# ACT copies the gate's products out of PSUM, and the sums of squares at the changes of layer go to TensorE

## The chip, the cores and the metric

The kernel runs on one core of a Trainium2 chip, in one launch. The metric is device time in microseconds (us), the median of three runs. The core has five engines that work beside each other, each through its own instructions in a fixed order: TensorE (PE in the profile; PEld is its weight load), VectorE (DVE), ScalarE (ACT), GpSimd (POOL), and SyncE (SP), which issues the DMAs. TensorE writes into PSUM, and DVE and ACT read it there.

## The reference

Two blocks follow one another on a sequence of 512 positions with 1024 channels. The first has two layers of feed-forward, mixer, feed-forward. The second has an even layer (rwkv, on 256 context positions and the 512 main ones) and an odd layer (retention). Cut to what the change touches:

```python
def rmsnorm(x, g):
    xf = x.astype(jnp.float32)
    y = xf * lax.rsqrt(jnp.mean(xf * xf, axis=-1, keepdims=True) + EPS)
    return (y * g.astype(jnp.float32)).astype(x.dtype)
...
# second_block, per layer; first_block ends each sublayer likewise
hl = rmsnorm(xl, norm_pre[layer]) * (1.0 + scale_l[:, None, :]) + shift_l[:, None, :]
hc = rmsnorm(xc, norm_pre[layer]) * (1.0 + scale_c) + shift_c
oc, ol = even_mixer(hc, hl, ...)      # odd_mixer in the odd layer
xl = xl + gate_l[:, None, :] * rmsnorm(ol, norm_post[layer])
if need_ctx:
    xc = xc + gate_c * rmsnorm(oc, norm_post[layer])
...
# even_mixer: u = h @ w_in gives r, k0, v, gate_r, four, gate_f
yr = o.astype(gate_r.dtype) * jax.nn.silu(gate_r)
yf = fourier_mix(four) * jax.nn.silu(gate_f)
return jnp.concatenate([yr, yf], axis=-1) @ w_out
```

## The kernel before

Channels lie on partitions: x is 8 tiles of 128x512, the context 8 tiles of 128x256 (`xc`). Every product runs in split precision: ACT copies a weight's high part (`whi`, L169), DVE subtracts to get the low part (`wlo`, L253), and three products are added up in PSUM (hi by hi, lo by hi, hi by lo; L174 records them all).

The **even layer** takes the most stages here. Its normed input is `ehh`/`ehl`, 768 columns wide (256 context, then 512 main). A projection of 128 channels (`project_in`, L999) fills one PSUM tile for the context columns (`ipc`, 128x256) and one for the main ones (`ipm`, 128x512). There is one buffer of each, so the next projection's first product into `ipc` waits until the last reader of this one has read. For each of six pairs of heads there are four projections: v, r and k0 (`shifted`, L1022, which lets ACT copy `ipc` and `ipm` into an SBUF tile `u` of 128x768, with one buffer, and mixes neighbours from there) and the gate (`project_gate`, L1347). The gate's silu is `sg = (tanh(g/2) + 1) * g`: ACT takes two tanh out of PSUM, and two DVE instructions add one and multiply by `ipc` and `ipm`, again out of PSUM. `sg` lies in one of the SBUF buffers that r, k and v share (tag `rkv`). Two more calls serve the Fourier channels, eight in all.

The recurrence itself runs in 12 slots, two directions for each pair. A slot's chain goes over all engines: a triangular inverse on DVE (`un`, `tmp`, L1508 to L1522: 28 short additions, each on the one before), a trip by DMA into `blocks`, transposes on DVE (`tn`, L1538), products `p`, `pb`, `ch` and so on. The projections (dense work) are laid between the chain's small products to fill TensorE. The order is set by a scheduler that plays the program on a timeline model when it is built, and then stands fixed on every engine.

At a **change of layer** the output y of a half (256 columns) is normed, scaled and added to x: `residual` (L389) does y's scaling on DVE (L188), the addition on POOL (L402), a square on ACT (`sq`) and, where a layer of the next block follows, the sum of squares on DVE (`sumsq`, L355: one addition of 128x256 into `xacc`, `xcacc` or `xkeep` for every tile but the first). The next layer's `norm_in` (L903) then calls `rstd_bc` (L331): products of the sum with ones into `st_ps`, ACT's square root, DVE's reciprocal, and products with the identity that spread the result over the partitions (`bc`). At the changes of sublayer within the first block `residual` already does it otherwise: each `sq` goes through products with ones into two PSUM columns (`xs`), with no addition on DVE. Such changes happen at about 420 us and later in the first block; the change from first to second block is near 2000 us, the one from the even to the odd layer near 2970 us.

Of the kernel before, what the change touches and what calls it, by code (L numbers as in the profile page):

```python
# [8 lines left out]
F32 = mybir.dt.float32  # L9
F32R = mybir.dt.float32r  # L10
AF = mybir.ActivationFunctionType
ALU = mybir.AluOpType
PSUM = bass.MemoryType.PSUM

D = 1024
KD = 8
# [132 lines left out]
class K:  # L149
# [236 lines left out]
        self.act(y[o][:, cols], ps[:, cols], AF.Copy)  # L386
        self.sumsq(yacc, ps[:, cols], o == 0, cols)

    def residual(self, x, y, yacc, c0, n, G, xacc=None, last=False):  # L389

        cols = slice(c0, c0 + n)
        bc = self.rstd_bc(yacc, c0, n, 1.0 / D, self.eps6)
        gates = list(zip(self.PEG, self.stats))
        sums = [self.paux("xs", *self.NST) for _ in range(2)] if xacc is None and not last else []
        done = None
        for k in range(KD + 1):
            if k < KD:
                with self.tc.issue_after(done.ins) if done and not self.POOLX else nullcontext():
                    self.stt(y[k][:, cols], y[k][:, cols], G[:, k : k + 1], bc[:, cols])
            if k:  # L400
                new = x[k - 1][:, cols]
                done = (self.nc.vector if last and k % 2 == 0 and (c0 or k > 4) else self.nc.gpsimd).tensor_tensor(out=new, in0=new, in1=y[k - 1][:, cols], op=ALU.add)  # L402
                if xacc is not None:
                    self.sumsq(xacc, new, k == 1, cols)
                elif last:
                    self.nc.sync.dma_start(self.A["out"][k - 1][:, cols], new)
                else:
                    sq = self.tp.tile([128, n], F32, tag=f"sq{n}", name="sq", bufs=self.NSQ)
                    self.act(sq, new, AF.Square)
                    for i, ps in enumerate(sums):  # L410
                        m = self.mm(ps[:, :1], sq[:, 128 * i : 128 * i + 128], self.ones, k == 1, k == KD)
                    gates.append((self.XEG[0] + int(self.XEG[1] * k), m))
        self.pe_gates = [] if last else gates
        return [ps[:, :1] for ps in sums]

    def boundary(self, x, out, G, nxt):
# [363 lines left out]
    def block1(self, stages, after):  # L780
# [75 lines left out]
        for i, (l, s) in enumerate(order):  # L856

            for n in order[i + 1 : i + 3] if s == 0 else order[i + 1 : i + 2] if s == 2 else ():
                self.bg += sum(ada(*n), [])
            if i + 1 == len(order):  # L860
                self.bg += after
            self.every = len(self.bg) / 27
            body = self.ffn(2 * l + s // 2) if s != 1 else (self.mixer_ab if l == 0 else self.mixer_c)
            out = body(hs)

            def G():
                if not gate:
                    self.flush()
                    g = self.cp.tile([128, 8], F32, tag="G", name="G", bufs=2)
                    self.stt(g, mods[(l, s)]["gate"], 1.0, self.vector("norm_post", 8, 8 * (3 * l + s)), ALU.add, ALU.mult)  # L870
                    if s != 1:
                        self.ts(g, g, 0.5)
                    gate.append(g)
                return gate[0]

            def nxt():
                if len(gate) < 2:
                    gate.append(mods_in(*order[i + 1]))
                return gate[1]

            gate = []
            if i + 1 < len(order):
                hs = self.boundary(self.x, out, G, nxt)
            else:
                self.xacc = self.xp.tile([128, 512], F32, tag="xacc", name="xacc")
                for c0, n in self.HALVES:
                    self.residual(self.x, *next(out), c0, n, G(), self.xacc)


    def ada2(self, l, mods):  # L890
# [12 lines left out]
    def norm_in(self, src, acc, g1, shift, hs, c0, halves):  # L903

        for o, n in halves:
            cols, dst = slice(o, o + n), slice(c0 + o, c0 + o + n)
            bc = self.rstd_bc(acc, o, n, 1.0 / D, self.eps6)
            for k in range(KD):
                t = self.t("hf")
                self.stt(t[:, cols], src[k][:, cols], g1[:, k : k + 1], bc[:, cols])  # L910
                hi, lo = hs[k]
                self.act(hi[:, dst], t[:, cols], AF.Identity, bias=shift[:, k : k + 1])
                self.stt(lo[:, dst], t[:, cols], shift[:, k : k + 1], hi.bitcast(F32)[:, dst], ALU.add, ALU.subtract)
# [20 lines left out]
    def even_layer(self):  # L934
# [8 lines left out]
        with tc.tile_pool(name="exc", bufs=1, reuse_waits="tile") as p:  # L943
            self.tp, self.NT = p, 4
            xc = self.load_ctx(p)
            cacc = p.tile([128, TC], F32, name="cacc")
            for k in range(KD):
                self.sumsq(cacc, xc[k], k == 0, slice(0, TC))
            self.norm_in(xc, cacc, g1c, mods["shiftc"], hs, 0, ((0, TC),))
            self.norm_in(self.x, self.xacc, g1l, mods["shiftl"], hs, TC, self.HALVES)  # L950
        xd = self.dp.tile([KD, 128, T], F32, name="xd")
        for k in range(KD):
            nc.sync.dma_start(xd[k], self.x[k])
# [11 lines left out]
        with tc.tile_pool(name="eo", bufs=1, reuse_waits="tile") as p:  # L965
# [4 lines left out]
            y.append(p.tile([128, CT], F32, name="oy"))  # L970
            yc, y = [t[:, :TC] for t in y], [t[:, TC:] for t in y]
            self.out_late(ins, y, yc, yacc, cacc, late, begun)
            self.xcacc = self.xp.tile([128, TC], F32, name="xcacc")
            self.residual(xc, yc, cacc, 0, TC, self.gated("Gc", mods["gatec"], 0, "Gc"), self.xcacc)
            self.xacc = self.xp.tile([128, T], F32, name="xkeep")
            G = self.gated("Gl", mods["gatel"], 0, "G")
            for c0, n in self.HALVES:
                self.residual(self.x, y, yacc, c0, n, G, self.xacc)
        ez_cm.__exit__(None, None, None)
        eh_cm.__exit__(None, None, None)  # L980
        self.xc = xc
# [365 lines left out]
    def project_gate(self, hs, S, p, key="sg", **place):  # L1347

        pc, pm = yield from self.project_in(hs, 20 + p)
        sg = self.e("sg", [self.CT], **(place or dict(tag="rkv", bufs=self.NRKV)))  # L1350
        self.act(sg[:, :TC], pc, AF.Tanh, scale=0.5)
        self.act(sg[:, TC:], pm, AF.Tanh, scale=0.5)
        self.stt(sg[:, :TC], sg[:, :TC], 1.0, pc, ALU.add, ALU.mult)
        self.stt(sg[:, TC:], sg[:, TC:], 1.0, pm, ALU.add, ALU.mult)
        S[key] = sg

    def prepare(self, S, p, d):
# [314 lines left out]
    def odd_layer(self):  # L1672
# [11 lines left out]
        for k in range(KD):  # L1684
            t = self.s(f"oc{k}", F32R)
            hc.append((t[:, :TC], t[:, TC:]))
        self.norm_in(self.xc, self.xcacc, g1c, mods["shiftc"], hc, 0, ((0, TC),))
        self.norm_in(self.x, self.xacc, g1l, mods["shiftl"], hs, 0, self.HALVES)
        con = self.sp.tile([128, OCON.n], F32, name="ocon")
        nc.sync.dma_start(con, A["ocon"])  # L1690
        C = lambda name, n: con[:, OCON.at[name] : OCON.at[name] + n]
# [213 lines left out]
    def program(self, first=True, second=True, stages=6):  # L1905
        nc, tc, A = self.nc, self.tc, self.A
        self.setup()
        with self.phase({"mm": ("mm", 4), "st": ("st", 2), "bc": ("bc", 2)}, (1024, self.NWS[0]), (4, 1), self.NSS):
# [6 lines left out]
            else:  # L1915
# [1 line left out]
                self.flush()  # L1917
                self.open_x()
                self.load_x()
                self.xacc = self.xp.tile([128, 512], F32, tag="xacc", name="xacc")  # L1920
                for k in range(KD):
                    self.sumsq(self.xacc, self.x[k], k == 0, slice(0, T))
        if second:
            with self.phase({"mm": self.INV, "st": ("seq", 1), "bc": ("y", 1)}, (512, self.NWS[1]), None):
                self.even_layer()
# [111 lines left out]
```

## Time and profile before

| | |
|---|---|
| runs | 3367.13, 3379.16, 3380.83 us; median 3379.16 |
| profiled execution | 3377.71 us, its span 3376.0 us |
| TensorE clock granted | 0.962 on the mean |
| busy share of the span | PE 94%, PEld 78%, DVE 54%, ACT 35%, POOL 9% |

A row of the timeline reads: start in us from the span's start, length in us, engine, line, operation, out<-in, shapes, count, and in brackets how long the engine had been idle before it and which instruction released it. A row of waits reads: engine, tile and line that waited, on whom, us in all, times, longest. In the windows each engine has its busy time and its instructions, PEclk is the granted clock as a share of full speed.

### The profile page before, as it was taken

To read this page: it belongs to the slowest core of one execution; us is meant where nothing else is said; L and a number is where in the kernel's file an instruction comes from. 1 tells how busy PE (TensorE), PEld (TensorE's weight loads), DVE (VectorE), ACT (ScalarE), POOL (GpSimd) and SP (SyncE) were. 2 spreads that over 40 slices of the span, in tenths; PEclk is the share of its full clock that TensorE was granted. 3 is DMA by queue.
4 is the path that set the end of the run, shared out by engine and by line. 5 is a ranking of instruction groups with operands and counts; after the bars stand their busy time and mean duration, and the time that the engine had idled before them with its cause. 6 is when DMAs were issued, how large, how long until landed. Compare 5 with 4: busy or idle time off the path is not lost. (4 is left out here: it accounts for less than half of the span.)

```text
span 3376.0 us, 58396 instructions
## 1 busy us (share of the span) xinstructions
PE 3165.4 (94%) x24530; PEld 2646.8 (78%) x24530; DVE 1834.4 (54%) x3336; ACT 1189.2 (35%) x1925; POOL 287.1 (9%) x285
## 2 busy tenths in 40 slices
PE   5999999999999999999999979999898899869998
PEld 4877887888889888878887868788787778758766
DVE  8554378444425554364667456456655655462554
ACT  4222244432223222344322234233332432242553
POOL 3000020200002000111000010011101111020000
PEclk8999999999999999999999989999999999979999
DMA  6555421144433554332355521211110111222112
GB/s 238 191 181 178 134 82 44 51 145 143 131 96 120 185 176 164 121 102 78 117 182 182 163 87 46 72 31 38 32 30 22 29 58 30 59 67 63 62 39 69
DMA packets 156503, 340.90 MB, mean 101 GB/s; under 512 B 52816, under 2 KB 64848, under 8 KB 156112
## 3 DMA queue, kind: packets, MB, share of 16 engines
q1 hardware_dynamic: 156240, 337.18, 30.8%
q8 instruction: 192, 3.15, 0.4%
q14 instruction: 71, 0.58, 0.1%
HBM read 328.20 MB, written 8.91 MB: 100 GB/s over the span
## 5 line engine op out<-in xcount | busy, mean ns | idle before, releaser
L169 ACT ACTIVATE whi<-raw 128x1024 fp32r<-128x1024 f32 (+2 forms) x451 | 426.0, 947 | 1122.1 <-PE po L174 266.4
L253 DVE TENSOR_TENSOR wlo<-raw,whi 128x1024 fp32r<-128x1024 f32 (+2 forms) x432 | 471.3, 1093 | 539.7 <-ACT whi L169 528.8
L313 DVE CUSTOM_DVE_ANT_0 raw_a<-raw_a,cond 128x1024 f32<-128x1024 f32 x176 | 215.4, 1230 | 339.2 <-DMA raw_a<-in_ada_w_dram 339.1
L174 PE MATMUL pu<-hh,whi 128*128 128x512 f32 (+1 forms) x824 | 317.5, 385 | 5.0 <-ACT whi L169 5.0
L174 PE MATMUL pu<-hh,wlo 128*128 128x512 f32 (+1 forms) x824 | 316.5, 384 | 2.9 <-DVE wlo L253 2.9
L174 PE MATMUL pu<-hl,whi 128*128 128x512 f32 (+1 forms) x824 | 316.2, 384 | 0.0
L174 PE MATMUL pg<-hh,whi 128*128 128x512 f32 (+1 forms) x752 | 293.6, 391 | 22.1 <-ACT hh L169 20.0
L174 PE MATMUL po<-ah,whi 128*128 128x512 f32 (+1 forms) x880 | 309.7, 352 | 3.0 <-ACT sq L169 3.0
L174 PE MATMUL po<-ah,wlo 128*128 128x512 f32 (+1 forms) x880 | 308.7, 351 | 0.0
L174 PE MATMUL po<-al,whi 128*128 128x512 f32 (+1 forms) x880 | 308.0, 350 | 0.0
L174 PE MATMUL pg<-hl,whi 128*128 128x512 f32 (+1 forms) x752 | 291.9, 389 | 5.2 <-DVE hl L188 5.2
L174 PE MATMUL pg<-hh,wlo 128*128 128x512 f32 (+1 forms) x752 | 292.3, 389 | 4.4 <-DVE wlo L253 4.2
L402 POOL TENSOR_TENSOR x<-x,y 128x256 f32<-128x256 f32 x106 | 77.2, 763 | 2107.7 <-DVE y L188 2107.4
L174 PEld LDWEIGHTS pg<-hh,whi 128*128 128x128 f32 x752 | 147.1, 196 | 53.7 <-ACT hh L169 22.2
L174 PEld LDWEIGHTS pu<-hh,whi 128*128 128x128 f32 x824 | 159.0, 193 | 37.4 <-ACT whi L169 5.8
L174 PEld LDWEIGHTS po<-ah,whi 128*128 128x128 f32 x880 | 166.2, 189 | 27.5 <-ACT sq L169 3.8
L174 PEld LDWEIGHTS pu<-hh,wlo 128*128 128x128 f32 x824 | 158.2, 192 | 36.1 <-DVE wlo L253 4.5
L174 PEld LDWEIGHTS po<-al,whi 128*128 128x128 f32 x880 | 166.2, 189 | 23.5
L174 PEld LDWEIGHTS po<-ah,wlo 128*128 128x128 f32 x880 | 166.2, 189 | 23.3
L174 PEld LDWEIGHTS pu<-hl,whi 128*128 128x128 f32 x824 | 158.6, 193 | 31.9
L174 PEld LDWEIGHTS pg<-hh,wlo 128*128 128x128 f32 x752 | 146.3, 195 | 37.5 <-DVE wlo L253 8.4
L174 PEld LDWEIGHTS pg<-hl,whi 128*128 128x128 f32 x752 | 146.0, 194 | 36.0 <-DVE hl L188 6.7
(468 smaller groups left out, 6507.5 us busy)
## 6 DMA issues: line engine op xcount, KB each, us to landing
raw<-in_w_dram SPq DMA_DIRECT2D x232, 512.0 KB, 4.1
raw_a<-in_ada_w_dram SPq DMA_DIRECT2D x176, 512.0 KB, 3.7
raw<-in_ev_in_dram SPq DMA_DIRECT2D x60, 256.0 KB, 2.6
raw<-in_w_dram SPq DMA_DIRECT2D x32, 384.0 KB, 3.6
raw_a<-in_ada_w_dram SPq DMA_DIRECT2D x32, 256.0 KB, 5.6
raw<-in_ab_in_dram SPq DMA_DIRECT2D x16, 512.0 KB, 3.2
raw<-in_ev_out_dram SPq DMA_DIRECT2D x20, 256.0 KB, 2.7
raw<-in_w_dram SPq DMA_DIRECT2D x16, 256.0 KB, 2.6
```

What stands on the lines that cost most here:

```text
L169: ins = self.nc.scalar.activation(out=out, in_=in_, func=func, scale=scale, bias=bias)
L174: self.last_mm = self.nc.tensor.matmul(out, lhsT=lhsT, rhs=rhs, start=start, stop=stop)
L253: (self.nc.gpsimd if self.nwt <= self.POOLW else self.nc.vector).tensor_tensor(out=lo, in0=src, in1=hi.bitcast(F32), op=ALU.subtract)
L313: self.nc.vector.tensor_tensor_reduce(out=out, in0=raw, in1=v, scale=1.0, scalar=0.0, op0=ALU.mult, op1=ALU.add, accum_out=dst[:, o : o + 1])
L402: done = (self.nc.vector if last and k % 2 == 0 and (c0 or k > 4) else self.nc.gpsimd).tensor_tensor(out=new, in0=new, in1=y[k - 1][:, col ...
```

## The change

Two edits, independent of each other.

In `project_gate`, ACT copies `ipc` and `ipm` into `u` (the same one-buffer tile that `shifted` uses), one tanh of 128x768 reads `u`, and one DVE instruction of 128x768 makes `sg` from `sg` and `u`.

In `residual`, where a `keep` is given (the end of the first block, the end of the even layer), the squares go through products with ones into `xs`, and square root and reciprocal are taken there, into `xrs` or `xcrs` (128 rows, one column for every 128 positions). `norm_in` then only spreads these over the partitions. The additions into `xacc`, `xcacc` and `xkeep` and the products `st_ps` of these go.

```diff
-    def residual(self, x, y, yacc, c0, n, G, xacc=None, last=False):
+    def residual(self, x, y, yacc, c0, n, G, keep=None, last=False):
...
-        sums = [self.paux("xs", *self.NST) for _ in range(2)] if xacc is None and not last else []
+        sums = [] if last else [self.paux("xs", *(self.NST if keep is None else self.NMM)) for _ in range(2)]
...
-                if xacc is not None:
-                    self.sumsq(xacc, new, k == 1, cols)
-                elif last:
+                if last:
                     self.nc.sync.dma_start(self.A["out"][k - 1][:, cols], new)
                 else:
                     sq = self.tp.tile([128, n], F32, tag=f"sq{n}", name="sq", bufs=self.NSQ)
                     self.act(sq, new, AF.Square)
                     for i, ps in enumerate(sums):
                         m = self.mm(ps[:, :1], sq[:, 128 * i : 128 * i + 128], self.ones, k == 1, k == KD)
-                    gates.append((self.XEG[0] + int(self.XEG[1] * k), m))
+                    if keep is None:
+                        gates.append((self.XEG[0] + int(self.XEG[1] * k), m))
         self.pe_gates = [] if last else gates
+        if keep is not None:
+            for i, ps in enumerate(sums):
+                self.act(keep[:, i : i + 1], ps[:, :1], AF.Sqrt, scale=1.0 / D, bias=self.eps6)
+            self.nc.vector.reciprocal(out=keep, in_=keep)
...
-            bc = self.rstd_bc(acc, o, n, 1.0 / D, self.eps6)
+            if isinstance(acc, tuple):
+                bc = self.paux("bc", *self.NBC)
+                for c in range(o, o + n, 128):
+                    self.mm(bc[:, c : c + 128], acc[0][:, c // 128 : c // 128 + 1].to_broadcast([128, 128]), self.con("ident", 128))
+            else:
+                bc = self.rstd_bc(acc, o, n, 1.0 / D, self.eps6)
...
-            self.norm_in(self.x, self.xacc, g1l, mods["shiftl"], hs, TC, self.HALVES)
+            self.norm_in(self.x, (self.xrs,), g1l, mods["shiftl"], hs, TC, self.HALVES)
...
         sg = self.e("sg", [self.CT], **(place or dict(tag="rkv", bufs=self.NRKV)))
-        self.act(sg[:, :TC], pc, AF.Tanh, scale=0.5)
-        self.act(sg[:, TC:], pm, AF.Tanh, scale=0.5)
-        self.stt(sg[:, :TC], sg[:, :TC], 1.0, pc, ALU.add, ALU.mult)
-        self.stt(sg[:, TC:], sg[:, TC:], 1.0, pm, ALU.add, ALU.mult)
+        u = self.e("u", [self.CT])
+        self.act(u[:, :TC], pc, AF.Copy)
+        self.act(u[:, TC:], pm, AF.Copy)
+        self.act(sg, u, AF.Tanh, scale=0.5)
+        self.stt(sg, sg, 1.0, u, ALU.add, ALU.mult)
         S[key] = sg
```

How the order moves, at three places. Numbers behind a name tell buffers' owners apart; "waits" names the engines on whose semaphores a row waits.

ACT, second slot of a pair in the even layer, around the third gate (`sg_21340` before, `sg_21362` in the changed kernel; `kd`, `L`, `DC`, `F` belong to the slot's chain, `ipc_21346` and `ipc_21369` are the next pair's k0 projection). Before:

```order
L169 ACTIVATE DC_19430<-L_19411 128x12 [waits DVE_49]
L169 ACTIVATE F_14993<-L_19411 128x12x64
L169 ACTIVATE kd_19412<-kd_19412,oka_14969,kah_14970 128x768 [waits DVE_49]
L169 ACTIVATE L_19411<-L_19411 128x768 [waits Activation_49,Pool_49]
L169 ACTIVATE sg_21340<-ipc_20627 128x256 [waits DVE_49]
L169 ACTIVATE sg_21340<-ipm_20628 128x512
L169 ACTIVATE whi_21934<-raw_21933 128x512 [waits DMAHW6_49,PE_49]
L169 ACTIVATE u_21963<-ipc_21346 128x256 [waits PE_49]
```

The same place in the changed kernel; the gate's own two copies into `u_21363` stand 27 rows further up, in the slot before:

```order
L169 ACTIVATE kd_19433<-kd_19433,oka_14987,kah_14988 128x768 [waits DVE_49]
L169 ACTIVATE L_19432<-L_19432 128x768 [waits Activation_49,Pool_49]
L169 ACTIVATE sg_21362<-u_21363 128x768 [waits DVE_49]
L169 ACTIVATE u_21986<-ipc_21369 128x256 [waits DVE_49]
L169 ACTIVATE u_21986<-ipm_21370 128x512 [waits PE_49]
L169 ACTIVATE g_19487<-p1_19488 128x512 [waits PE_49]
L169 ACTIVATE g_19487<-p1_19506 128x256 [waits PE_49]
```

The tanh has kept its place behind the slot's `kd` and `L`. The copy of the next projection stands right behind it and waits for DVE.

DVE at that place, before:

```order
L183 TENSOR_TENSOR kd_19412<-kd_19412,k0_17903 128x768 [waits Activation_49]
L194 TENSOR_SCALAR kk_20192<-k0_19624,vec_60 128x768 [waits DVE_49]
L183 TENSOR_TENSOR o_19449<-kd_18566,kd_19412 128x768 [waits DVE_49]
L188 SCALAR_TENSOR_TENSOR sg_21340<-sg_21340,ipc_20627 128x256 [waits Activation_49]
L188 SCALAR_TENSOR_TENSOR sg_21340<-sg_21340,ipm_20628 128x512 [waits Activation_49]
L188 SCALAR_TENSOR_TENSOR sq_19450<-r_18660,vec_60,o_19449 128x768 [waits DVE_49]
```

And in the changed kernel:

```order
L253 TENSOR_TENSOR wlo_22001<-raw_21999,whi_22000 128x512 [waits DMAHW7_49,PE_49,Activation_49]
L194 TENSOR_SCALAR kk_20214<-k0_19646,vec_60 128x768 [waits DVE_49]
L183 TENSOR_TENSOR kd_19433<-kd_19433,k0_17924 128x768 [waits Activation_49]
L183 TENSOR_TENSOR o_19470<-kd_18587,kd_19433 128x768 [waits DVE_49]
L188 SCALAR_TENSOR_TENSOR sg_21362<-sg_21362,u_21363 128x768 [waits Activation_49]
L188 SCALAR_TENSOR_TENSOR sq_19471<-r_18681,vec_60,o_19470 128x768 [waits DVE_49]
```

The gate's DVE work stands where it stood, behind the chain's `kd` and `o`; at this gate a weight's subtraction has come in ahead of them.

TensorE (PE) at that place, before; `wl` and `alm` are the last products of the chain ahead of the projection:

```order
L174 MATMUL wl_19416<-tw_14996,w2t_18560 128x512 [waits Activation_49]
L174 MATMUL alm_19417<-al_14997,a2t_18561 128x512 [waits Activation_49]
L174 MATMUL ipc_21346<-ehh0_14760,whi_21223 128x256 [waits DVE_49]
L174 MATMUL ipc_21346<-ehl0_14761,whi_21223 128x256
L174 MATMUL ipc_21346<-ehh0_14760,wlo_21224 128x256
```

And in the changed kernel, where `ipc_21997` is the projection after it (v):

```order
L174 MATMUL alm_19438<-al_15015,a2t_18582 128x512 [waits Activation_49]
L174 MATMUL ipm_21370<-ehh6_14802,whi_21372 128x512
L174 MATMUL ipm_21370<-ehl6_14803,whi_21372 128x512
L174 MATMUL ipm_21370<-ehh6_14802,wlo_21373 128x512
L174 MATMUL ipm_21370<-ehh7_14804,whi_21372 128x512
L174 MATMUL ipm_21370<-ehl7_14805,whi_21372 128x512
L174 MATMUL ipm_21370<-ehh7_14804,wlo_21373 128x512
L174 MATMUL ipc_21997<-ehh0_14790,whi_21957 128x256 [waits Activation_49]
```

The projection that waited for DVE has moved ahead of the wait, most of it into the slot before; the projection behind it now stands at that place and waits for ACT.

## Rows read from the trace of the kernel before

**Rows 1.** The page: busy time, share of the span, instructions.
```profile
PE 3165.4 (94%) x24530; PEld 2646.8 (78%) x24530; DVE 1834.4 (54%) x3336; ACT 1189.2 (35%) x1925; POOL 287.1 (9%) x285
```

**Rows 2.** Waits of PE: total us, times, longest.
```profile
PE ipc L174 <- DVE sg L188: 32.2, 4, 10.4
...
PE p L174 <- DVE tn L1538: 4.3, 2, 2.2
```

**Rows 3.** Timeline of PE around the third gate.
```profile
2419.10 0.59 PE L174 MATMUL alm<-al,a2t 64*128 64x512 f32 x1
2430.11 0.58 PE L174 MATMUL ipc<-ehh,whi 128*128 128x256 f32 x1 [10.42 <-DVE sg L188]
...
2438.46 1.61 PE L174 MATMUL p<-tn,am 64*64 64x64 f32 x48
```

**Rows 4.** Windows behind that stall: length, then PE, PEld, DVE, ACT, POOL, PEclk.
```profile
2430.00:2434.50 4.50, 4.39 (x20) 4.40 (x21) 1.84 (x4) 0.00 (x0) 4.47 (x6) 0.50 0.24 22
2434.50:2438.40 3.90, 3.90 (x19) 3.12 (x17) 1.10 (x3) 0.69 (x2) 0.00 (x0) 0.90 0.00 0
```

**Rows 5.** Timeline of DVE in that stall.
```profile
2417.86 0.17 DVE L183 TENSOR_TENSOR tmp<-un 96x14 f32<-96x14 f32 x1
...
2427.38 0.95 DVE L183 TENSOR_TENSOR kd<-kd,k 128x768 f32<-128x768 f32 x1
...
2428.77 0.95 DVE L183 TENSOR_TENSOR o<-kd 128x768 f32<-128x768 f32 x1
2429.64 0.41 DVE L188 SCALAR_TENSOR_TENSOR sg<-sg,ipc 128x256 f32<-128x256 f32 x1
...
2434.47 1.04 DVE L1538 STREAM_TRANSPOSE tn<-blocks 128x512 f32<-128x512 f32 x2 [2.66 <-DMA blocks<-ad]
2438.30 0.69 DVE L253 TENSOR_TENSOR wlo<-raw,whi 128x512 fp32r<-128x512 f32 x1 [2.79 <-PE ipc L174]
```

**Rows 6.** Timeline of ACT there.
```profile
2428.36 0.38 ACT L169 ACTIVATE sg<-ipc 128x256 f32<-128x256 f32 x1 [0.44 <-DVE kd L183]
...
2438.34 0.38 ACT L169 ACTIVATE u<-ipc 128x256 f32<-128x256 f32 x1
```

**Rows 7.** Instructions on tile sg: ns min/median/max, first and last start.
```profile
L188 DVE SCALAR_TENSOR_TENSOR sg<-sg,ipc x8: 405/410/423, 2117.9 to 2711.5; 128x256 f32<-128x256 f32 x8
...
L188 DVE SCALAR_TENSOR_TENSOR o<-o,lb,sg x6: 1018/1019/1019, 2357.7 to 2944.5; 128x768 f32<-128x768 f32 x6
```

**Rows 8.** Timeline of PE at a change of sublayer, with xs.
```profile
424.98 0.28 PE L174 MATMUL po<-ah,wlo 128*128 128x256 f32 x1
425.10 0.50 PE L174 MATMUL xs<-ones,sq 128*128 128x1 f32 x4
425.46 0.36 PE L174 MATMUL po<-ah,whi 128*128 128x256 f32 x1
425.67 0.28 PE L174 MATMUL po<-al,whi 128*128 128x256 f32 x1
```

**Rows 9.** Timeline of DVE, ACT and PE from first to second block.
```profile
1999.97 4.06 DVE L183 TENSOR_TENSOR xacc<-xacc,sq 128x256 f32<-128x256 f32 x6
...
2006.20 0.42 ACT L169 ACTIVATE cacc<-xc 128x256 f32<-128x256 f32 x1 [3.06 <-DMA xc<-in_ctx_dram]
...
2012.39 1.01 PE L174 MATMUL st_ps<-ones,xacc 128*128 128x1 f32 x4 [0.35 <-ACT r L169]
2013.27 0.99 PE L174 MATMUL bc<-cst,r 128*128 128x128 f32 x3
```

**Rows 10.** Timeline of POOL and DVE from even to odd layer.
```profile
2967.89 6.05 POOL L402 TENSOR_TENSOR xc<-xc,oy 128x256 f32<-128x256 f32 x8 [91.38 <-DVE oy L188]
2973.90 14.18 POOL L402 TENSOR_TENSOR x<-x,oy 128x256 f32<-128x256 f32 x16
...
2985.77 3.13 DVE L183 TENSOR_TENSOR xkeep<-xkeep,sq 128x256 f32<-128x256 f32 x4
2988.81 1.65 DVE L188 SCALAR_TENSOR_TENSOR hf<-xc,g1c,bc 128x256 f32<-128x256 f32 x4
```

More of the change, by code (lines that the diff above doesn't have):

```diff
@@ L884, in block1 @@
             else:
-                self.xacc = self.xp.tile([128, 512], F32, tag="xacc", name="xacc")
+                self.xrs = self.xp.tile([128, 4], F32, name="xrs")
                 for c0, n in self.HALVES:
-                    self.residual(self.x, *next(out), c0, n, G(), self.xacc)
+                    self.residual(self.x, *next(out), c0, n, G(), self.xrs[:, c0 // 128 : (c0 + n) // 128])
     def ada2(self, l, mods):
@@ L972, in even_layer @@
             self.out_late(ins, y, yc, yacc, cacc, late, begun)
-            self.xcacc = self.xp.tile([128, TC], F32, name="xcacc")
-            self.residual(xc, yc, cacc, 0, TC, self.gated("Gc", mods["gatec"], 0, "Gc"), self.xcacc)
-            self.xacc = self.xp.tile([128, T], F32, name="xkeep")
+            self.xcrs = self.xp.tile([128, 2], F32, name="xcrs")
+            self.residual(xc, yc, cacc, 0, TC, self.gated("Gc", mods["gatec"], 0, "Gc"), self.xcrs)
+            self.xrs = self.xp.tile([128, 4], F32, name="xrs")
             G = self.gated("Gl", mods["gatel"], 0, "G")
             for c0, n in self.HALVES:
-                self.residual(self.x, y, yacc, c0, n, G, self.xacc)
+                self.residual(self.x, y, yacc, c0, n, G, self.xrs[:, c0 // 128 : (c0 + n) // 128])
         ez_cm.__exit__(None, None, None)
@@ L1686, in odd_layer @@
             hc.append((t[:, :TC], t[:, TC:]))
-        self.norm_in(self.xc, self.xcacc, g1c, mods["shiftc"], hc, 0, ((0, TC),))
-        self.norm_in(self.x, self.xacc, g1l, mods["shiftl"], hs, 0, self.HALVES)
+        self.norm_in(self.xc, (self.xcrs,), g1c, mods["shiftc"], hc, 0, ((0, TC),))
+        self.norm_in(self.x, (self.xrs,), g1l, mods["shiftl"], hs, 0, self.HALVES)
         con = self.sp.tile([128, OCON.n], F32, name="ocon")
@@ L1919, in program @@
                 self.load_x()
-                self.xacc = self.xp.tile([128, 512], F32, tag="xacc", name="xacc")
-                for k in range(KD):
-                    self.sumsq(self.xacc, self.x[k], k == 0, slice(0, T))
+                raise NotImplementedError
         if second:
```

## The prediction

> **What bounds the kernel now.** I read the page's busy shares first: TensorE is busy for 94% of the span, DVE for 54%, ACT for 35% [rows 1]. So a saving on DVE or ACT is worth only what it takes off a wait of TensorE, and the next view is what TensorE waits for. The longest entry there is the one the first edit aims at: the first product into `ipc` waits for the gate's DVE work, 32.2 us in four times, the longest 10.4 [rows 2]. Three of the four are equal, at the third, fourth and fifth gate; the last is what is left of the sum, 32.2 less three times 10.4, about 1 us, at a Fourier gate.
>
> The timeline around the third gate shows what such a stall is made of. TensorE begins its last product of the chain at 2419.10 and the next projection at 2430.11, after 10.42 us idle [rows 3]. [...]
>
> Why does it wait? Not because PSUM is read slowly. DVE is in the chain's inverse from 2417.86, then come `kd` at 2427.38 and `o` at 2428.77, and only then, at 2429.64, the gate's first instruction [rows 5]. Its input, ACT's tanh, starts at 2428.36, released by DVE's `kd` [rows 6]: `kd` is the last reader of the buffer that `sg` gets. The gate is late because its SBUF buffer comes free late and because it stands behind the chain on DVE.
>
> **The gate.** Removed are, for each of eight gates, two tanh out of PSUM and two DVE instructions of 0.41 and 0.68 us; added are two ACT copies, one tanh and one DVE instruction of 128x768 with both operands in SBUF. The trace has one of that shape, `o<-o,lb,sg`, at 1.02 us [rows 7], against 1.09 for the pair: nothing gained on DVE. ACT gains a copy of 0.38 [rows 6] and one like it for the wider half, in an engine that is idle for two thirds of the time; this costs nothing unless it stands in the chain.
>
> Does the stall go? The copies empty `ipc` and `ipm` early now, in the slot before, and k0's projection moves ahead of the stall. But the order in the section on the change shows that the tanh still stands behind `kd` and `L`, and the DVE instruction still behind `o`. `u` has one buffer. So the copy of k0's projection into `u` waits for the gate's DVE instruction, and the projection after it, v's, waits for that copy. The stall moves on by one projection. The projections' products are the same in all, so I count TensorE's idle time alone.
>
> Fourth and fifth gate, where DVE's order has not changed: before, TensorE went on when the first DVE instruction had ended, 2429.64 + 0.41 = 2430.05. Now it goes on when the whole one has, and a copy: 1.02 - 0.41 + 0.38 and a few hundredths for the semaphore = 1.05 us later, twice: +2.1. What the earlier k0 products pay back: in the first slots of these two pairs TensorE waited twice, 4.3 us together, for the transposes `tn` [rows 2], and k0's products now fill these waits: -4.3.
>
> Third gate: the projection's rest, 20 products, runs behind the chain's last product; 19 took 3.9 us [rows 4], so TensorE stops near 2423. In the changed order DVE has a weight's subtraction more (0.69 at 2438.30 [rows 5]; 0.6 net of its overlap) and does the three scans behind the inverse, not within it, which I put at 1.2 us, from the gaps between the inverse's short instructions. The gate ends at 2429.64 + 1.8 + 1.0 = 2432.4, the copy at 2432.9: idle 9.9 instead of 10.4, -0.5. First, second and Fourier gates: a projection of other work lies between the gate and the next use of `u`, 8.35 us (2430.11 to 2438.46 [rows 3]): 0, at most 1 us either way.
>
> Gates in all: 2.1 - 4.3 - 0.5 = -2.7 us; each of the three slow stretches stays. Not shown by the trace is how far the scheduler's other moves in these slots cost or save; I bound them by half a projection either way, 4 us.
>
> [...]
>
> **From first to second block.** In the first half's `residual` TensorE is busy with the second half's products (`po`), and the 16 products with ones are put among them. Four such passes lie between two `po` at 424.98 and 425.67, which are 0.69 us apart, two spacings of 0.12 without them [rows 8]: 0.45 us for each of eight tiles, +3.6 us, uncovered. In the second half TensorE is idle, and its 16 cost nothing in themselves. There the six additions, 4.06 us from 1999.97 [rows 9], make way for products, two roots and a reciprocal on the tail of the same squares; then comes the context's load, whose first tile ACT waits for until 2006.20 [rows 9]. It may start up to 0.6 us later. On the other side `bc` no longer follows the products of `xacc` with ones: 2013.27 - 2012.39 = 0.9 us earlier [rows 9]. Together -0.3, bounds -0.9 and +0.6; in all +3.3.
>
> **From even to odd layer.** TensorE waits for a chain of POOL's additions and DVE. POOL's first eight take 6.05 us, 0.76 each, the next sixteen 14.18, 0.89 each [rows 10], while DVE does its additions beside them. Without those I expect 0.76 throughout, so POOL ends near 2967.9 + 24 * 0.76 = 2986.1 instead of 2988.1. Square, products, two roots and a reciprocal follow, which I estimate at 1.9 us: 0.42 for a square [rows 9], twice 0.50 at most for the products at the lower clock [rows 8], the rest for the three short ones. So the first `hf` starts near 2988.0 instead of 2988.81 [rows 10], and the last addition no longer stands between the `hf`, 0.7 by the 3.13 us that four took [rows 10]: -1.5. Bounds: -3 if POOL runs faster yet, +0.5 if it stays at 0.89.
>
> **Sum.** -2.7 + 3.3 - 1.5 = -0.9 us. The profiled execution took 3377.71 us, 1.7 beside its span, and stands 1.45 below the median of 3379.16. From it the sum gives 3376.8, from the median 3378.3; I forecast 3377.
>
> **Rivals.**
> First, faster: the stalls go. For it: the PSUM tiles are released in the slot before. Against it: `u` has one buffer, and its release is the instruction that PSUM waited for until now. Gone whole, it is worth three idle stretches of 10.4 and three slow ones of 2.0, 37 us, and with the other terms some 3341; half gone, 3359.
>
> Second, slower: `u` as a bottleneck. Behind the gate k0's copy, its six mixing instructions on DVE, then v's copy have to pass through `u` one after another, before r's projection may begin. I estimate 1.5 us of slack there. Behind the chain's next products `p` DVE has two additions or transposes and the last mixing to do, 0.4 to 0.7 us each as its rows of such widths [rows 5], and ACT a copy of 0.38 [rows 6]: some 2.1 us. TensorE meanwhile has ten products at 0.2 and one more round of `p` at 1.6 [rows 3, 4]: 3.6 us. If the chain on DVE puts the mixing off by more, TensorE loses up to one projection of 8.35 us at each of three places: +25, 3402. Against it is that k0's mixing stands closer behind the transposes than before.
>
> Third, the stall moves, but the sums miss: the 16 products cost double at the first change of block, or the odd layer's start is not earlier. That is up to +5, and still no change.
>
> **Chances.** The stall moves on and nothing changes: 0.62, own range 3369 to 3387. First rival, half or whole: 0.23. Second: 0.15. A measurement of this kernel can tell some 0.5%, 17 us, from no change; half a stall gone is just beyond it. So faster 0.23, same 0.62, slower 0.15. The range goes from 3351, which leaves out the whole of the first rival, to 3392, which leaves out the whole of the second.
>
> **What would show it.** In the changed profile TensorE's wait for `sg` should be gone from the list of waits, and in its place stand a wait of `ipc` (and of `eoc` or `eom` at the fifth gate) for ACT's `u`, three times, of 10 to 11.5 us, with `u<-ipc` itself waiting for DVE's `sg`. Behind each the clock should again be at 0.50 for some 4 us. The two waits for `tn` should be gone. `xs` should show 80 instructions more, and the 16 at the first change of block a last `po` 3 to 4 us later. The forecast is wrong if the waits for `u` are short (first rival) or if there are more of them than three, with other projections than the next one (second).

## The result, and the profile after

The changed kernel takes 3401.3 us (median of 4), the kernel before 3379.1 beside it: ratio 1.0077 [1.0058, 1.0096], 22 us slower. The forecast was 3377. The profiled execution took 3400.43 us, 22.7 more than the profiled one before. In it no engine has grown much by the page (busy us, share, instructions):

```profile
PE 3197.4 (94%) x24670; PEld 2671.3 (79%) x24670; DVE 1811.3 (53%) x3293; ACT 1198.9 (35%) x1938; POOL 287.7 (8%) x285
```

Against [rows 1], TensorE has 140 instructions and 32 us more: 160 passes of `xs` (480 against 320), two for each of the 80 products, less 20 others. 140 passes would take 17 us at the 0.12 that neighbours stand apart where the granted clock is 1.00 (424 to 426 before), so part of the 32 is products that ran slower. What TensorE waits for (total us, times, longest):

```profile
PE ipc L174 <- ACT u L169: 24.3, 5, 11.4
...
PE eoc L174 <- ACT u L169: 11.4, 1, 11.4
PE hbc L174 <- ACT rt L169: 6.3, 2, 4.8
...
PE pw L174 <- DVE gk L183: 2.7, 2, 1.9
```

The wait for `sg` [rows 2] is gone, and `u` stands in its place, as forecast. The third gate again, as in [rows 3, 5, 6], on TensorE, ACT and DVE:

```profile
2447.34 0.39 PE L174 MATMUL ipm<-ehh,wlo 128*128 128x512 f32 x1
2456.24 0.58 PE L174 MATMUL ipc<-ehh,whi 128*128 128x256 f32 x1 [8.51 <-ACT u L169]
```
```profile
2453.00 0.84 ACT L169 ACTIVATE sg<-u 128x768 f32<-128x768 f32 x1 [0.99 <-DVE kd L183]
2455.80 0.39 ACT L169 ACTIVATE u<-ipc 128x256 f32<-128x256 f32 x1 [1.96 <-DVE sg L188]
```
```profile
2452.02 0.95 DVE L183 TENSOR_TENSOR kd<-kd,k 128x768 f32<-128x768 f32 x1
2453.00 1.37 DVE L183 TENSOR_TENSOR o<-kd 128x768 f32<-128x768 f32 x1
2454.29 1.48 DVE L188 SCALAR_TENSOR_TENSOR sg<-sg,u 128x768 f32<-128x768 f32 x1
```

The chain is the forecast's: tanh behind `kd`, DVE's gate behind `o`, the next projection's copy behind the gate, TensorE behind the copy.

Where the 22.7 us arose is read from landmarks that occur in every kernel: the same instruction's start, after less before.

| from | to | after | forecast |
|---|---|---|---|
| start | a `po` of the last sublayer of block 1 (1914 before) | -0.2 | 0 |
| there | first `hf` of the even layer (2014.50 before) | +6.8 | +3.3 |
| there | first `p` of the first slot (2157.35) | +6.0 | 0 |
| there | 97th of the 192 `p` of the last slot (2907.68) | +6.9 | -2.7 |
| there | first `pv` of the odd layer (2996.25) | +5.8 | -1.5 |
| there | end | -2.5 | 0 |

All four stretches for which I had a term, or should have had one, missed, and to the same side. The fourth row, from the first slot's first `p` to the last slot's 97th, is called the stretch of the slots below.

### The profile page after: what moved, and what is told of

It reads as the page before. It is cut to its first block, busy times and chain, and to the rows that moved or that the text cites. A ratio compares the mean times of both kernels' runs of the same rounds, so it can differ in the third digit from the quotient of the medians.

```text
span 3398.7 us, 58641 instructions
## 1 busy us (share of the span) xinstructions
PE 3197.4 (94%) x24670; PEld 2671.3 (79%) x24670; DVE 1811.3 (53%) x3293; ACT 1198.9 (35%) x1938; POOL 287.7 (8%) x285
```

## The experiments

Times are medians beside runs of the kernel before (3375.6 to 3379.5 in the four sets); the ratios have 95% intervals.

### The two edits apart

The gate's edit alone, and the sums' edit alone, each as in the diff of the change.

> The kernel before with the gate's edit alone. Theory (the loss is a sum of parts that do not need each other): the even layer from its second pair on costs what it costs in the changed kernel, where the distance to the kernel before grows from 12.6 to 19.4 us; so +4 to +7 us, 3383 to 3386, TensorE waiting three times for ACT's u, 8 to 11.5 us each, in place of three waits of 10.4 for DVE's sg, and nothing lost in the first pair's slot. Rival (the forecast's own sum for the gates): -2.7, 3376. Rival 2: the gate edit brings nearly all of it: +20, 3399.

> The kernel before with the sums of squares by products with ones alone. Theory: +6.6 us at the end of the first block (8 x 4 passes between the po products, 3.6 us at full clock, and some 3 us more because the granted clock falls to 0.5 behind them while TensorE is busy), +5.4 in the first slot of the even layer (DVE's gk behind the start of the inverse in the fixed order), +3.5 at the odd layer's start (96 passes at 0.21 us one behind the other): +15, 3394. Rival (the forecast's sum: passes at full clock, none that counts where TensorE was idle): +1.8, 3381.

Gate alone: 3399.7 us, 1.0057 [1.0040, 1.0074]. Sums alone: 3403.9, 1.0073 [1.0053, 1.0094]. Alone the one costs 20 us and the other 24 (its profiled run, 3397.3, is the fastest of its four), and together they cost 22: they don't add. The gate's time is that of its second rival, which had the gate bring nearly all of the loss; the sums' is above its theory's 3394. The edits touch different code, but they meet in the one fixed order. The stretch of the slots shows where the gate's loss goes. Before, and with the gate alone (length, then TensorE busy with its instructions, PEld, DVE, ACT, POOL, clock):

```profile
2157.35:2907.68 750.33, 688.96 (x11931) 607.74 (x11931) 443.99 (x1055) 262.50 (x459) 98.55 (x93) 0.95 0.14 37
```
```profile
2156.97:2930.42 773.45, 698.65 (x11931) 608.75 (x11931) 445.08 (x1050) 267.64 (x465) 103.91 (x93) 0.95 0.14 36
```

The same 11,931 products take 23.1 us longer: 13.4 idle (74.8 against 61.4) and 9.7 busy. The three waits for `u` are not it: 8.27, 11.37 and 11.37 us, together 31.0, replace three for `sg` of 31.3. New are others: `hbc` for `rt` 14.5 us in all instead of 5.7, `ipc` for `whi` 4.4. The first `hbc` that waits for over 4 us, on TensorE, and ACT and DVE ahead of it:

```profile
2526.87 1.18 PE L174 MATMUL hbc<-cst,rt 128*128 128x128 f32 x4 [4.50 <-ACT rt L169]
```
```profile
2521.48 0.22 ACT L169 ACTIVATE DC<-L 128x12 f32<-128x12 f32 x1 [4.04 <-DVE L L1389]
...
2523.75 0.18 ACT L169 ACTIVATE hr<-hst 128x12 f32<-128x12 f32 x1
...
2525.99 0.82 ACT L169 ACTIVATE rt<-hr 128x768 f32<-128x768 f32 x1
```
```profile
2519.49 0.18 DVE L183 TENSOR_TENSOR un<-un,tmp 96x26 f32<-96x26 f32 x1
2519.60 1.85 DVE L1389 TENSOR_TENSOR_SCAN L<-ec,sig 128x256 f32<-128x256 f32 x3
```

ACT's `rt` is made from `hr`, and `hr` stands behind `DC`, which waits for the scans `L`. On DVE the scans stand behind 26 of the inverse's 28 additions, with r's mixing among these. Before, ACT had `hr` ahead of `DC`, DVE had the scans behind 24 of the 28 and r's mixing behind all of them, and this `hbc` did not wait. ACT at that place before:

```profile
2506.35 0.18 ACT L169 ACTIVATE hr<-hst 128x12 f32<-128x12 f32 x1
...
2507.84 0.22 ACT L169 ACTIVATE DC<-L 128x12 f32<-128x12 f32 x1
```

### The gate with a tile of its own, and controls

```diff
-        u = self.e("u", [self.CT])
+        u = self.e("u", [self.CT], tag="gu")
...
-            us = self.e("us", [4, 64], bufs=5)
+            us = self.e("us", [4, 64], bufs=4)
```

`us4` has only the second line, in the kernel before. `rkv8` has it and `NRKV = 8` for 7, so that the gate (unchanged there) finds a buffer before `kd` is done.

> The gate's edit alone, with a tile of its own for the gate's copy, so that the next projection's copy does not wait for the gate's DVE instruction (its 3 KB are paid for by one buffer less of the chain's us, 4 in place of 5). Theory (the single u holds the stall): the three waits of 8.5 to 11.4 us for u<-ipc go, and the slow stretches behind them: -20 to -37, 3342 to 3359. Rival (buffers of k0, v and r and DVE's place for their mixing hold it as well, so that v's copy waits for k0's mixing): the waits come back one projection later, within 3 us of gate_only.

> The kernel before with 4 buffers of the tile us instead of 5, nothing else: the control for the gate with a tile of its own, which took that buffer for its room. Theory: us is not waited for, so 3378.5 to 3381 us, and the 19 us that the own tile gave against the gate edit alone are all of the tile. Rival: the fifth buffer matters or its loss moves the order for the better or worse, a difference of more than 3 us either way; then the own tile's result is read against this one.

> The kernel before, gate as it was, with 8 buffers of the tag rkv instead of 7 (and us 4 instead of 5 for the room, which by itself changed nothing: 1.0001), so that the third and fourth gate find an SBUF buffer before kd is done. Theory: PE's waits of 10.4 us are for that buffer, so the third and fourth go; but in the gate edit with its own tile the place of such a wait was taken by the next pass's own tn on DVE (4.8 and 10.4 us), so what is won is at most part of it: 5 to 15 us, 3364 to 3374, and the fifth gate, which has a buffer of its own place, keeps its 10 us. Rival 1 (nothing takes their place): 2 x 11 us and the half clock behind them won, 3352 to 3358. Rival 2 (DVE's fixed chain is what bounds these passes, and the stalls are only where PE meets it): within 3 us of before, 3376 to 3382, with waits for tn of about 10 us in their place.

Own tile: 3380.6, 1.0004 [0.9993, 1.0015]; control: 3379.2, 1.0001 [0.9989, 1.0014]. So with a tile of its own the gate's edit costs nothing, but it gains nothing either; both theories missed. The third and fourth gate with the own tile, on TensorE:

```profile
2446.56 2.63 PE L174 MATMUL p<-tn,am 64*64 64x64 f32 x48 [4.81 <-DVE tn L1539]
...
2581.80 2.82 PE L174 MATMUL p<-tn,am 64*64 64x64 f32 x48 [10.41 <-DVE tn L1539]
```

At these two the projection no longer waits, and the slot's own `p` waits for DVE's transposes instead. At the fifth gate `eoc` still waits for `u`, 11.4 us, as in the whole change. The waits of `hbc` for `rt` are 5.7 us again, as before. `rkv8` says the same from the other side: 3382.1, 1.0020 [1.0010, 1.0030], where 3364 to 3374 was expected. Its second rival, by which DVE's chain is the bound, named what came, though one of the two waits is for `u`, and the time is 6.5 us over the 3375.6 beside it, not within 3:

```profile
2443.94 1.33 PE L174 MATMUL p<-tn,am 64*64 64x64 f32 x20 [7.34 <-DVE tn L1538]
...
2582.82 0.58 PE L174 MATMUL ipc<-ehh,whi 128*128 128x256 f32 x1 [15.29 <-ACT u L169]
```

Taking the buffer's wait away gave none of the 10.4 us back: at these places the chain on DVE and ACT sets when TensorE goes on, whatever it waits for by name. What the own tile saves against the gate alone in the stretch of the slots, 754.7 us against 773.5, is 16.5 us of waits and 2.2 of slower products. Whether sharing `u` makes them by itself, or the order that it leads to, isn't settled, since a tile of its own changes both.

### The sums with wide products

```diff
-  self.mm(ps[:, :1], sq[:, 128 * i : 128 * i + 128], self.ones, k == 1, k == KD)
+  self.mm(ps[:, :128], sq[:, 128 * i : 128 * i + 128], self.ones.to_broadcast([128, 128]), k == 1, k == KD)
```

(at the changes of layer only.) `sums_wide` is the sums alone, `after_wide` the whole change, `own_wide` the whole change with the gate's own tile.

> As the last, but each product with ones has 128 equal columns instead of one (the first column is used). Theory (the clock falls because passes of one column leave TensorE with little to do while it counts as busy): the granted clock stays at 1.0 through the po products at the end of the first block and rises in the 96 passes before the odd layer, which then take 0.12 us each and not 0.21; +3.6 to +4.5 there and -1.5 to 0 at the odd layer: +2 to +5, 3381 to 3384, in spite of more columns. Rival (what counts is the number of passes and weight loads, not their columns): as sums_only or slower, the clock again at 0.5 behind the products: +10 or more at these two places.

> The change whole, but each of the sums' products at the changes of layer writes 128 equal columns (the ones broadcast) instead of one; nothing else differs. Theory (the change has two causes that do not share a place: TensorE's clock under the one-column products, and the gates' copies that stand for a buffer of u): the first is gone, the second stays, so the time is that of the gate edit alone, 3397 to 3402 us against 3379.5 before; the granted clock is 1.00 during the last output products of the even layer, the first hf comes about 3 us later than before instead of 6.6, and the three long waits for ACT's u (8 to 11.5 us) stand where they stood. Rival (the two edits meet, since the loss of the whole change, 22.7, is far less than 20 + 19): with the sums at no cost the gates' loss comes out otherwise too, under 3395 or over 3405.

> The change whole with both causes taken away: the sums' products 128 columns wide, and the gate's copies in a tile of their own (tag gu, with one buffer fewer of us, 5 to 4, to make room) instead of u. Theory: 3378 to 3383 us, no change that can be told from the kernel before: the wide sums alone gave ratio 1.0000, the gate with its own tile 1.0004. Rival (the cost lies in the edits' moved order, not in the tile u and not in the one column): 3395 or more, since both orders move again here.

Sums: 3379.6, 1.0000 [0.9990, 1.0009]. Whole change: 3392.0, 1.0045 [1.0028, 1.0061], below what the theory gave and within its rival: the two edits meet, and the gate's loss isn't the same with other sums. Whole change with own tile: 3384.5, 1.0021 [1.0011, 1.0031], between the two theories. So here 128 columns cost less than one (the sums alone 3379.6 against 3403.9). But this edit, too, had changed DVE's order, and the next two experiments part that from the clock.

### The odd layer's sums alone, one column and 128

The change from the even to the odd layer alone, in `late_wide` with 128 columns and in `late_one` with one. Up to the last `xs` TensorE, DVE and POOL have the same order in both; on ACT the two roots of x's first half stand two squares further down with one column.

> The kernel before with only the sums of the change from the even to the odd layer by products, 128 columns wide; the change from the first to the second block and the gate are as before. Theory: the wide sums lost 2.85 us at the change of block and won 2.6 at the start of the odd layer, so this one, which keeps only the gain, is 2 to 3.5 us faster than before: 3375.5 to 3377.5 against 3379.5, with the same place up to the end of the even layer. Rival (the gain at the odd layer's start was a drift between profiles, or PE there is the bound): within 1 us of before, 3378.5 to 3380.5.

> Only the change from the even to the odd layer has the sums by one-column products; gate and block change as before. Up to the last xs every engine has the order of the run that had the same sums 128 columns wide there (ratio 0.9998). Theory: with one column the granted clock stays at 0.50 while TensorE is busy, the passes take 0.21 us each instead of about 0.13, and from the last p of the even layer to the odd layer's first hf 4 to 6 us are lost (with 128 columns 2.3 were won): 3383 to 3387 against 3378. Rival (the clock is at 0.50 there for another reason, and the products hide): within 2 us of the wide run.

128 columns: 3377.2, 0.9998 [0.9989, 1.0007]. One column: 3382.0, 1.0015 [1.0005, 1.0024]. From the last slot's 97th `p` to the odd layer's first `hf` the one is 2.3 us faster than before, the other 5.9 slower, each as its theory had it for that stretch. In the whole time the gain of `late_wide` doesn't show: 0.7 us, within its rival's 1, and within the interval. One column, then 128 (TensorE's timeline, and windows as above):

```profile
2972.78 2.72 PE L174 MATMUL xs<-ones,sq 128*128 128x1 f32 x12 [1.18 <-ACT sq L169]
...
2976.36 5.97 PE L174 MATMUL xs<-ones,sq 128*128 128x1 f32 x28
...
2983.19 11.95 PE L174 MATMUL xs<-ones,sq 128*128 128x1 f32 x56
```
```profile
2980.00:2985.00 5.00, 5.00 (x25) 5.00 (x25) 1.73 (x5) 2.33 (x7) 3.68 (x6) 0.50 0.00 0
2985.00:2990.00 5.00, 5.00 (x25) 5.00 (x25) 1.82 (x6) 2.84 (x8) 4.50 (x7) 0.50 0.01 2
```
```profile
2972.09 2.93 PE L174 MATMUL xs<-ones,sq 128*128 128x128 f32 x12 [1.19 <-ACT sq L169]
...
2975.59 3.39 PE L174 MATMUL xs<-ones,sq 128*128 128x128 f32 x28
...
2979.67 8.88 PE L174 MATMUL xs<-ones,sq 128*128 128x128 f32 x56
```
```profile
2980.00:2985.00 5.00, 5.00 (x35) 4.11 (x33) 3.26 (x9) 3.40 (x10) 5.00 (x8) 1.00 0.01 2
```

With one column TensorE is busy without a gap from 2980 to 2990 and its clock stays at 0.50: 0.21 us a pass (11.95 / 56), 20.6 for 96. With 128 columns the first twelve passes are as slow (2.93 us, against 2.72), then the clock rises to 1.00, and 28 take 3.39, 0.12 each. TensorE's busy time does not tell the two apart: from 2980 to 2985 it is 5.00 of 5.00 in both, at 0.50 in the one and at 1.00 in the other. Why the clock rises in one alone isn't shown.

### The block change's sums alone, and the order behind it

The change from the first to the second block alone: `block_one` with one column, `block_16` with 16 equal ones. The first has DVE's order of the whole change here, with the inverse's first additions (`tmp`, `un`) ahead of both `gk`; the second has both `gk` first, as before. Up to the first `hf` the two kernels have the same order on every engine, and from there to the first `p` they differ on DVE alone, at this place.

> Only the change from the first to the second block has the sums by one-column products; gate and odd layer as before. DVE's fixed order has here, as in the whole change, the first un of the pass ahead of the second gk. Theory: the last po some 6.6 us late (3.6 of products, 3 of the half clock), the first p of the even layer 12 us late, with the 5 to 6 us between them from that order (PE's pw waits for gk, then half clock); the end 8 to 13 us late, 3387 to 3392. Rival (the 5 to 6 us come from the lateness itself, since the un wait for a DMA that starts later): the same here, but then also in the run with 16 columns.

> As the run of the change of block alone, but each of its sums' products writes 16 equal columns. DVE's fixed order has here both gk ahead of the first un, as in the kernel before. Theory: whatever the 16 columns do to the clock at the change of block (a last po 3.6 us late if it stays at full clock, 6.6 if not), no more is lost from there to the first p of the even layer than 1 us: the first p is 3 to 7.5 us late. Rival (the loss in the first pass is not from the order): another 5 to 6 us there, the first p 9 to 13 us late.

One column: 3395.4, 1.0060 [1.0040, 1.0080]. Sixteen: 3380.3, 1.0019 [1.0009, 1.0029]. The first `hf` comes at about the same place in both (2.54 and 2.58 us later than before, 3.3 and 4.1 counted from the `po` at 1914), and from there to the first `p` the one loses 7.1 us, the other 0.5. That was the theory for this place, and the rival, by which the lateness itself costs it, is out. The time of `block_one` is over its forecast of 3387 to 3392 all the same. DVE in the whole change, then with 16 columns:

```profile
2102.89 0.17 DVE L183 TENSOR_TENSOR tmp<-un 96x14 f32<-96x14 f32 x1 [6.98 <-DMA un<-ad]
2103.10 0.18 DVE L183 TENSOR_TENSOR un<-un,tmp 96x14 f32<-96x14 f32 x1
2103.20 0.68 DVE L183 TENSOR_TENSOR gk<-pg,ec 128x512 f32<-128x512 f32 x1
```
```profile
2097.98 0.69 DVE L183 TENSOR_TENSOR gk<-pg,ec 128x512 f32<-128x512 f32 x1 [1.91 <-PE pg L174]
2099.25 0.17 DVE L183 TENSOR_TENSOR tmp<-un 96x14 f32<-96x14 f32 x1 [0.58 <-DMA un<-ad]
```

In the whole change `gk` is queued behind an instruction that waits for a DMA, and TensorE's `pw` waits for `gk`, then runs slowly, at a clock of 0.50 (2108 to 2112): 1.12 us for 16, where the 16 at 2105.38 took 0.68:

```profile
2107.97 1.12 PE L174 MATMUL pw<-vt,gk 64*64 64x64 f32 x16 [1.91 <-DVE gk L183]
```

The loss doesn't end there. In the stretch of the slots, with gate and products as before, one column and 16:

```profile
2166.98:2925.53 758.55, 693.90 (x11931) 607.31 (x11931) 445.34 (x1055) 263.40 (x459) 99.23 (x93) 0.96 0.14 37
```
```profile
2160.48:2908.74 748.26, 684.31 (x11932) 602.23 (x11931) 444.29 (x1055) 262.72 (x459) 99.94 (x93) 0.96 0.14 37
```

10 us apart in another fixed order. How far profiles of one order differ can be read too: the kernel before, `us4`, `late_wide` and `late_one` have the same order in this stretch and take 750.3, 749.5, 751.9 and 748.2; `block_one`, its repeat and `sums_only` share another and take 758.6, 757.8 and 757.0. So the order is worth some 8 us here, beyond what profiles of one order differ by. One wait tells them apart: `ipc` waits 4.3 us for `whi` near 2520 in all three, 2.1 in `block_16`, and not at all in the other four. In the whole change this stretch takes 757.2, in `after_wide` 763.7, in `own_wide` 751.1.

A third form of the sums adds the squares on DVE and has only two products for each half:

> The sums at the changes of layer alone, gate as before: squares still on ACT, but added up on DVE (7 additions for each half) and only then 2 products of one column for each half (instead of 16 in each), and the root and reciprocal as in the change. Theory (the sums' loss of 19 us is the price of the one-column products, at full and at half clock, and of the order behind them): without 14 of 16 products the change of block costs nothing (first hf within 1 us of before; the last po as before), and the odd layer's start is as before or up to 2 us earlier: 3376 to 3380. Rival (the loss is in where root and reciprocal stand in ACT's and DVE's order): it stays, 3390 or more.

It took 3389.9, 1.0045 [1.0030, 1.0060]; the theory missed, and the time is its rival's. The first `hf` came 0.1 us earlier, counted from the `po` at 1914, as forecast; but the stretch of the slots took 758.7, 8.4 more, in an order of its own, though no product of the sums lies in it. In the odd layer `xs` waited for the additions, and the first `hf` came 3.7 us later than before, counted from the last slot's 97th `p`:

```profile
3000.71 1.01 PE L174 MATMUL xs<-ones,kacc 128*128 128x1 f32 x4 [7.78 <-DVE kacc L183]
```

### The clock at the block change, once more

In the whole change the granted clock fell among the last `po`; in `block_one`, in the same order of TensorE's instructions, it did not (windows of the one, then of the other):

```profile
1986.00:1990.00 4.00, 4.00 (x31) 4.00 (x30) 0.00 (x0) 1.30 (x4) 0.72 (x2) 0.78 0.00 0
1990.00:1993.00 3.00, 3.00 (x16) 3.00 (x16) 0.59 (x2) 1.57 (x6) 0.00 (x0) 0.50 0.00 0
1993.00:1996.00 3.00, 3.00 (x19) 3.00 (x19) 1.29 (x2) 0.60 (x2) 0.00 (x0) 0.66 0.30 107
```
```profile
1986.00:1990.00 4.00, 4.00 (x37) 4.00 (x37) 0.42 (x1) 1.64 (x5) 0.32 (x1) 1.00 0.00 0
1990.00:1993.00 3.00, 3.00 (x27) 3.00 (x27) 1.46 (x3) 1.37 (x4) 0.00 (x0) 1.00 0.13 18
```

> The whole change once more, for its profile alone: does the granted clock fall to 0.50 among the last po of the block again? Theory (the one-column products bring the clock to an edge, and a profile falls on either side of it: the whole change and the sums alone fell, the run with the block change alone didn't, in the same order of TensorE's instructions): either; with the clock down the first hf is 6 to 7 us late, without it 3 to 4. The gates' three waits of 8.5, 11.4 and 11.4 us stand as before, within 0.3 us. Rival (it always falls here): 0.50 in some 5 us of 1986 to 1996 again.

> The block change's sums alone once more, for its profile alone. Theory (an edge): the clock may fall this time; the wait of pw for gk and 6 to 7 us from the first hf to the first p come again in any case, since the order is fixed. Rival (the clock never falls in this kernel, so something else of the whole change is needed): 1.00 again from 1980 to 1997.

The repeats took 3404.8 and 3391.3 us and did each as its first did: 0.50 again in the whole change, first `hf` 6.6 us late, counted from the `po` at 1914; 1.00 again in `block_one`, 3.4 late, and 7.0 more to the first `p`. Two profiles of each don't rule chance out, and what decides it stays open: up to there the two kernels have the same order on every engine. With one column the clock fell in three of five profiles (`sums_only` too, for half as long; its first `hf` is 4.8 late), with 128 in none of three (1.00 from 1982 to 1996 in `sums_wide`, `after_wide` and `own_wide`).

## Why the prediction was wrong

**The gates' stalls: right.** Forecast were waits of 9.9, 11.5 and 11.5 us for `u`; they are 8.5, 11.4 and 11.4, in the places named. Of the two waits for `tn`, 4.3 us, which the sum had as gone, one of 1.8 us is left. The slow stretches behind the stalls, which the sum leaves as they are and the first rival has at 2.0 us each, are an estimate of mine; no run shows what one costs by itself. The traces show the spacing of products of 256 columns: before, 0.21 us behind the third gate at a clock of 0.50 (4.43 us from 2430.11 to 2434.54 for 20), 0.12 where it is 1.00 (2437.60 to 2438.10); in the changed kernel 0.21 again, for 2.9 us behind the third gate (2456.24 to 2459.18) and 3.6 behind the fourth (2588.71 to 2592.29), where 4 were forecast.

**"Not shown by the trace is how far the scheduler's other moves ... cost or save; I bound them by half a projection either way, 4 us": this step failed.** The stretch of the slots takes from 748.2 to 773.5 us over these kernels, with the same products. The gate's edit, priced at -2.7, took +23.1 there alone and, with the sums, +6.9. And the way to the first slot's `p`, which no term of the sum named, lost 6.0 through `gk` behind `un`. The gate's term counted the places that it changes on purpose; the order moved in the other slots too. Which moves make the 23.1 is shown for the longest new waits only.

**The block change: price right, clock missed.** 3.3 us were forecast, and `block_one` gave 3.3 and 3.4; its last `po` came 3.8 late, with 3.6 forecast. In the whole change the clock fell besides, for some 3.4 more.

**The odd layer: the failed step is "twice 0.50 at most for the products".** It priced the passes on the tail of the last square and left out that 96 of them stand in one queue at half clock, 20.6 us, with `bc` between them. POOL did become faster, as said, and behind its end the first `hf` and the first `pv` came late:

```profile
2987.51 5.52 POOL L402 TENSOR_TENSOR xc<-xc,oy 128x256 f32<-128x256 f32 x8 [92.66 <-DVE oy L188]
2993.11 5.52 POOL L402 TENSOR_TENSOR x<-x,oy 128x256 f32<-128x256 f32 x8
2999.94 5.51 POOL L402 TENSOR_TENSOR x<-x,oy 128x256 f32<-128x256 f32 x8 [1.31 <-DVE oy L188]
```
```profile
3012.25 1.66 DVE L188 SCALAR_TENSOR_TENSOR hf<-xc,g1c,bc 128x256 f32<-128x256 f32 x4 [0.67 <-PE bc L174]
...
3021.47 0.79 PE L174 MATMUL pv<-whi,oh 128*128 128x512 f32 x1 [3.08 <-ACT oh L169]
```

POOL takes 0.69 for each, against 0.76 and 0.89 [rows 10], and all 24 take 2.2 us less, with 2.0 forecast. But from its end to the first `hf` it is 6.8 us where the sum had 1.9, because the products end last. And from there to the first `pv` it is 9.2 us, 7.4 before: the sum had 0.7 saved there, and 1.8 were lost. With 128 columns the first of these comes right: 1.8 us from POOL's end to the first `hf`, and this `hf` 2.3 earlier, with 0.8 forecast. The second stays at 9.2, so at the first `pv` 0.5 is left of a forecast 1.5. It is the fixed order once more: ACT does `zeta` and `xi` ahead of `oh`, which `pv` waits for, and did them behind its first two before. ACT in `late_wide`, then before:

```profile
2995.78 0.87 ACT L169 ACTIVATE zeta<-lgam,ocon 128x8 f32<-128x8 f32 x4
...
2997.79 1.69 ACT L169 ACTIVATE oh<-hf,shiftl 128x256 fp32r<-128x256 f32 x4
```
```profile
2996.47 0.51 ACT L169 ACTIVATE oh<-hf,shiftl 128x256 fp32r<-128x256 f32 x1 [0.28 <-DVE hf L188]
...
2998.30 0.68 ACT L169 ACTIVATE zeta<-lgam,ocon 128x8 f32<-128x8 f32 x3
```

**The slower rival named the wrong cause.** Its place, later projections waiting for `u` for up to a whole projection, doesn't occur: the long waits are the three forecast, and of the others the longest is 2.7 us. Its 3402 is near the time by accident. The faster rival's 3341 and 3359 should be 3342 and 3361 by the prediction's own terms; nothing rests on the difference.

No version here beats the kernel before beyond its interval; `late_wide`, 0.9998, comes nearest.

## What to carry to other kernels

Where the order is fixed by a scheduler, an edit is priced over every stretch in which the order moved: look for an instruction that now stands behind one that waits for a DMA or for another engine. A wait that is removed is worth nothing while the chain behind it is as late (`rkv8`). And small products aren't free on an idle TensorE: here 96 one-column passes at a clock of 0.50 formed a queue of 20.6 us, in which the clock didn't rise.

## What the runs showed of the hardware

The granted clock stayed at 0.50 through 20 us (2975 to 2995 in `late_one`) in which TensorE was busy without a gap, with 84 one-column float32 passes and eight of 128 columns (`bc`). In three profiles of five (`after`, `after_again`, `sums_only`) it fell from 1.00 to 0.50 among output products with one-column passes between them. With 128 columns in their place, at the odd layer (`late_wide`), it rose behind the first twelve passes, to 0.95 from 2975 to 2980 and 1.00 from 2980, and a pass of 128 columns was then cheaper than one of a single column at 0.50: 0.12 against 0.21 us.
